# Projections of a dilated-attention step with written orders of loads, VectorE, ScalarE and TensorE

## The chip, the cores and the metric

The kernel runs on one core of a Trainium2 chip. The metric is the device time of one execution in microseconds, lower is better.

## The reference

One inference step of a decoder trunk of two layers over 512 prompt rows and 64 sample rows (8 sequences of 8 positions). The stage that matters here is the start of the first layer:

```python
h = rmsnorm(x, p['norm_mix'][i])
qkv = (h @ w_qkv).reshape(B, T, 3, N_DIL, N_HEAD_SLOTS, HEAD_DIM)   # 1024 -> 3 x 3 x 512
q = rope(rmsnorm(qkv[:, :, 0], q_gain), pos)
k = rope(rmsnorm(qkv[:, :, 1], k_gain), pos)
v = qkv[:, :, 2]
```

There are three head groups with window and dilation (128, 1), (512, 4) and (2048, 16). The sample rows also score against cached keys of each group (`cache_kv_w128`, `cache_kv_w512`, `cache_kv_w2048`). Attention, an output projection, a feed-forward block, a state-space layer and a second feed-forward block follow; they are not edited.

## The kernel before

All products are made in a split form: a weight tile `raw` is turned into a high part `whi` (a copy on ScalarE, L100) and a low part `wlo` (a subtraction on VectorE, L101), and three products on TensorE (high by high, low by high, high by low) add up to nearly full precision.

`qkv_phase` makes nine chunks of 512 columns: q2, k2, v2, q1, k1, q0, k0, v0, v1 (the digit is the group). A chunk is made by `qkv_chunk` in four steps (`kk`), each with a quarter of the depth: one weight load of 512 KB, one split, and 28 products of 512 columns into five accumulator banks (four of prompt rows, one of sample rows). The steps are numbered 0 to 35 by `turn[0]`. Behind each of the five groups of products of a step is a slot, `slot()`, where work that was put off with `later(n, fn)` is issued, n slots after it was asked for.

After a q or k chunk, the banks are evicted and scaled by ScalarE (L573; the sample rows by `sample_rows`, L377 and L378), squares (L577) and sums (L578) give the roots (L119 and `newton`, L110 to L114), and `finish(t)` rotates one of five row tiles on VectorE (L589, L591, L592). `turned(t)` then transposes it on TensorE (L604) and copies it out (L610). The rotations are spread over the next chunk's steps by `LATE` and `LAST`.

Beside this, cached keys are scored for the sample rows. Group 2 works by VectorE: for each of 32 pairs (sequence, part), `products` loads a key tile and a broadcast query tile from the scratch `qscr` and multiplies and reduces them (L409, L410); after four parts `Close2.turn` transposes the result into the score bank `Sd` (L427, L430) and VectorE adds the mask (L432). Groups 1 and 0 work by TensorE: `Score.turn` transposes one key unit (L516), ScalarE copies it (`ks`, L518), and `Score.dots` multiplies (L527, L532) into `Sd`, followed by VectorE's mask step (L534). `Sd` has one buffer, the transposes' bank `pt` two, the key copies `ks` two, and the cached tiles `kc` six.

The order on each engine comes from a planner that orders instructions by its own estimates of their times, except where `keep_in_program_order` ties an instruction to the one tied before it on the same engine. In the kernel before, the products and transposes on TensorE are tied from step 20 on (`PINNED`), and nothing else in this stage is. `PLAN` says behind which step the cached pairs and scores are asked for: in `step()`, at the end of a step, the tiles are loaded and their work is issued at once.

## Time and profile before

| | us |
|---|---|
| median of 3 runs | 1535.78 (1533.81 to 1536.32) |
| profiled execution, its own time | 1540.19 |
| span of the profiled execution | 1538.4 |
| first product of the second chunk | 40.48 |
| last product of the stage starts | 332.7 |

In the rows that follow, a timeline row has the start, the duration, the engine, the line of the code, the operation, what it writes and reads, and in brackets the engine's idle time before it with what ended it. A row of stretches has the stretch, its length, then for TensorE, its weight loads, VectorE, ScalarE and GpSimd the busy time and the number of instructions, the granted TensorE clock, the busy share of the DMA engines and GB/s; where it was asked for one line of the code, it has that line's engines alone. A row of groups has busy time and mean duration in ns, then idle time before, and a row of waits has who waited for whom, the total, the number and the longest. A row of DMA issues has the count, the size and the median time to landing.

### The profile page before, as it was taken

How to read it: one execution, taken by the hardware profiler on the slowest of the kernel's cores; microseconds unless marked ns; L12 is line 12 of the kernel's file. 1: busy time of each engine (PE TensorE's matmuls, PEld its weight loads, DVE VectorE, ACT ScalarE, POOL GpSimd, SP SyncE). 2: the span in 40 equal slices, each digit the busy share in tenths (PEclk: the TensorE clock that was granted, in tenths of full speed). 3: DMA queues.
4: the chain of work that ended last, by engine and by line, in shares of the span. 5: the costliest groups of instructions: out<-in, count | busy, mean ns of one | idle time of the engine just before them, and what ended most of it. 6: DMA issues, size and time to landing. Idle time of an engine off the chain costs nothing. (4 is left out here: it accounts for less than half of the span.)

```text
span 1538.4 us, 29552 instructions
## 1 busy us (share of the span) xinstructions
PE 1485.8 (97%) x12406; PEld 1391.0 (90%) x12406; DVE 902.7 (59%) x1507; ACT 521.2 (34%) x790; POOL 321.3 (21%) x368
## 2 busy tenths in 40 slices
PE   9999897898999999999999999999999999999998
PEld 7778675666799999999999999999999999999998
DVE  5899776444556954488789567853543333333342
ACT  4533444445544221222222353532332212221222
POOL 2012231220012107554344330030110001000100
PEclk9999999899999999999999999999999999999999
DMA  7599466788965655778766947965556555442222
GB/s 258 189 347 324 124 223 208 221 293 299 313 185 192 219 198 192 246 262 285 246 226 212 328 138 220 292 198 172 192 191 217 191 190 190 148 147 83 83 68 77
DMA packets 190493, 322.63 MB, mean 210 GB/s; under 512 B 39480, under 2 KB 137016, under 8 KB 188824
## 3 DMA queue, kind: packets, MB, share of 16 engines
q1 hardware_dynamic: 182888, 303.76, 58.9%
q10 hardware_dynamic: 4992, 10.04, 1.9%
q0 software_dynamic: 2480, 6.95, 1.2%
q8 instruction: 97, 1.59, 0.4%
q14 instruction: 36, 0.29, 0.1%
HBM read 289.22 MB, written 118.78 MB: 265 GB/s over the span
## 5 line engine op out<-in xcount | busy, mean ns | idle before, releaser
L101 DVE TENSOR_TENSOR wlo<-raw,whi 128x1024 fp32r<-128x1024 f32 x200 | 247.7, 1238 | 251.7 <-ACT whi L100 248.2
L100 ACT ACTIVATE whi<-raw 128x1024 fp32r<-128x1024 f32 x200 | 208.1, 1042 | 526.3 <-PE acc L107 407.6
L107 PE MATMUL acc<-xgl,whi 128*128 128x288 f32 x1760 | 379.0, 296 | 1.0 <-DVE xgl L172 1.0
L107 PE MATMUL acc<-xgh,wlo 128*128 128x288 f32 x1760 | 377.3, 295 | 0.0
L107 PE MATMUL acc<-xgh,whi 128*128 128x288 f32 x1760 | 377.1, 296 | 0.1
L107 PEld LDWEIGHTS acc<-xgl,whi 128*128 128x128 f32 x1760 | 282.6, 188 | 2.5 <-DVE xgl L172 1.3
L107 PEld LDWEIGHTS acc<-xgh,wlo 128*128 128x128 f32 x1760 | 282.9, 188 | 0.8 <-DVE wlo L101 0.4
L107 PEld LDWEIGHTS acc<-xgh,whi 128*128 128x128 f32 x1760 | 281.5, 188 | 0.7 <-DVE gt L906 0.3
L908 POOL TENSOR_TENSOR gt<-gt,rstd 128x576 f32<-128x576 f32 x44 | 77.2, 1756 | 430.4 <-ACT gt L907 430.3
L107 PE MATMUL acc<-hh,whi 128*128 128x288 f32 x704 | 151.3, 296 | 0.0
L107 PE MATMUL acc<-hh,wlo 128*128 128x288 f32 x704 | 151.1, 295 | 0.0
L107 PE MATMUL acc<-hl,whi 128*128 128x288 f32 x704 | 150.9, 295 | 0.0
L338 PE MATMUL acc<-wlo,xh 128*128 128x512 f32 x288 | 114.5, 399 | 2.8 <-DVE wlo L101 2.8
L338 PE MATMUL acc<-whi,xh 128*128 128x512 f32 x288 | 113.4, 415 | 1.3 <-ACT xh L277 1.1
L107 PEld LDWEIGHTS acc<-hh,wlo 128*128 128x128 f32 x704 | 113.0, 188 | 0.2 <-issue 0.2
L107 PEld LDWEIGHTS acc<-hl,whi 128*128 128x128 f32 x704 | 112.9, 188 | 0.2 <-issue 0.2
L107 PEld LDWEIGHTS acc<-hh,whi 128*128 128x128 f32 x704 | 113.0, 188 | 0.0
L338 PE MATMUL acc<-whi,xl 128*128 128x512 f32 x288 | 112.6, 398 | 0.0
L192 POOL TENSOR_TENSOR ssum<-ssum,sq 128x576 f32<-128x576 f32 x21 | 35.8, 1703 | 235.9 <-ACT sq L191 235.9
L338 PEld LDWEIGHTS acc<-wlo,xh 128*128 128x128 f32 x288 | 55.6, 193 | 14.5 <-DVE wlo L101 4.3
L338 PEld LDWEIGHTS acc<-whi,xh 128*128 128x128 f32 x288 | 55.2, 193 | 12.9 <-ACT xh L277 1.7
L409 DVE TENSOR_TENSOR kc<-kc 128x1024 f32<-128x1024 f32 x32 | 39.0, 1219 | 45.9 <-DMA kc<-qscr 45.9
(361 smaller groups left out, 1951.5 us busy)
## 6 DMA issues: line engine op xcount, KB each, us to landing
o_kv_s<-cache_kv_w SPq DMA_DIRECT2D x64, 1020.0 KB, 7.3
kc<-cache_kv_w SPq DMA_DIRECT2D x96, 512.0 KB, 5.8
raw<-ffn_w_gate SPq DMA_DIRECT2D x44, 512.0 KB, 4.1
raw<-ffn_w_up SPq DMA_DIRECT2D x44, 512.0 KB, 3.8
raw<-ffn_w_down SPq DMA_DIRECT2D x40, 512.0 KB, 3.5
raw<-w_qkv SPq DMA_DIRECT2D x36, 512.0 KB, 5.5
kc<-qscr SPq DMA_DIRECT2D x32, 512.0 KB, 6.1
o_kv_s<-cache_kv_w SPq DMA_DIRECT2D x16, 1008.0 KB, 6.1
```

The costliest lines, as they stand in the source:

```text
L100: s.activation(hi, raw, AF.Copy)
L101: mark[0] = v.tensor_tensor(lo, raw, hi.bitcast(F32), OP.subtract)
L107: te.matmul(ps[:, c, :HN], w, x[:, c * HN:(c + 1) * HN], start=first and i == 0, stop=last and i == 2)
L192: g.tensor_tensor(self.ss, self.ss, sq, OP.add)
L338: ins = nc.tensor.matmul(*a, **kw)
L409: eng.tensor_tensor(kc, kc, qb, OP.mult)
L908: g.tensor_tensor(t, t, nin.r, OP.mult)
```

## The change

The order on SyncE's loads, VectorE, ScalarE and TensorE in this stage is written out. `v` and `s` are wrapped in `Kept`, so that each of their instructions is tied in program order; TensorE is tied from the second chunk on; the loads of weights and cached tiles are tied too. What a step issues ahead of its products stands in a new function `begin()`:

1. the weight load of two steps ahead, the cached pairs of the next step, the key tiles of this step's scores (and in step 34 the next stage's values and masks);
2. the split of the next step's weights;
3. the work listed for the step: in the first step after a q or k chunk the roots and the first rotated tile, then the other rotations;
4. the products of the pairs whose tiles were asked for a step ago.

`Score` objects are made at the end of the step, from tiles that are already asked for. The squares and sums move from the eviction of a chunk to step 3 of this list. The table `PLAN` becomes `PAIRS` and `SCORES`, with some pairs at other steps (none in steps 8, 16, 17 and 20, two in 12 to 15 and 32 to 34). `turned(t)` comes 9 - t // 2 slots after the start of the step of its rotation, `Close2.turn` 10 slots after the start of its step. The store to `qscr` goes from SyncE's queue to GpSimd's.

```diff
-LATE, LAST = (2, 1, 1, 1), (2, 2, 1, 0)
-PLAN = {5: (2,), 6: (2,), ... 12: (2, 2), 13: (2,), 14: (2, 2), ... 20: (2,), 21: (1, 2), ... 32: (0, 0, 2, 2), 33: (0, 2), 34: (0, 0, 2)}
+CHUNKS = ((0, 2), (1, 2), (2, 2), (0, 1), (1, 1), (0, 0), (1, 0), (2, 0), (2, 1))
+LATE, LAST = (1, 2, 1, 1), (2, 2, 1, 0)
+PAIRS = {6: 1, 7: 1, 9: 1, 10: 1, 11: 1, 12: 2, 13: 2, 14: 2, 15: 2, 18: 1, 19: 1, 21: 1, ... 31: 1,
+         32: 2, 33: 2, 34: 2}
+SCORES = {21: (1,), ... 28: (1,), 29: (0,), 30: (0,), 31: (0,), 32: (0, 0), 33: (0,), 34: (0, 0)}
...
+    kept = tc.keep_in_program_order
+    v, s = Kept(tc, v), Kept(tc, s)
...
+    def begin():
+        j = turn[0]
+        if 4 <= j + 2 < 36:
...
+            kept(nc.sync.dma_start(raw, dram(A["w_qkv"], ...)))
+            raws.append(raw)
+        due = [ready.pop(0) for _ in range(PAIRS.get(j, 0))]
+        for _ in range(PAIRS.get(j + 1, 0)):
+            b, part = fill[2].pop(0)
+            kc = cache_tile(nc, A, kst, "kc", 2, b, 2 * part, 2, 0, kept)
+            qb = kst.tile([128, 2, 512], F32, name="kc")
+            kept(nc.sync.dma_start(qb, dram(qscr, ...)))
+            ready.append((b, part, kc, qb))
+        for gi in SCORES.get(j, ()):
+            b, n = fill[gi].pop(0), UNITS[gi]
+            cached.append((gi, b, [cache_tile(nc, A, kst, "kc", gi, b, c0, min(2, n - c0), 0, kept) for c0 in range(0, n, 2)]))
+        if j in notes:
+            notes[j]()
+        if j < 4:
+            split(j)
+        if j >= 3:
+            split(j + 1)
+        for fn in works.pop(j, ()):
+            fn()
+        for b, part, kc, qb in due:
...
+            v.tensor_tensor(kc, kc, qb, OP.mult)
+            v.tensor_reduce(...)
+            if part == 3:
+                later(10, Close2(nc, L, v, dk, psd, "Sd", prods.pop(b), b).turn)
+        return splits.pop(0)
...
+        def roots():
+            sh = wk.tile([128, 5, 8], F32, name="sh")
+            v.memset(sh[64:128, 4], 1.0)
+            for t in range(5):
+                pp = 128 if t < 4 else 64
+                sq = wk.tile([128, 8, 64], F32, name="t1")
+                s.activation(sq[:pp].rearrange("p h d -> p (h d)"), at[t][:pp], AF.Square)
+                v.tensor_reduce(sh[:pp, t], sq[:pp], AX.X, OP.add)
+            rsqrt(rq, sh, 1.0 / HD)
...
-            if turn[0] < PINNED:
-                turned(t, a, pp)
-            else:
-                later(4, lambda: turned(t, a, pp))
+            if (gi, part, t) == (2, 0, 4):
+                g.dma_start(qscr, a[:64])
+            later(9 - t // 2, lambda: turned(t, a, pp))
...
+        order = [4, 0, 1, 2, 3]
+        works[turn[0]] = [roots]
+        for i, n in enumerate(LATE if turn[0] < 28 else LAST):
+            works.setdefault(turn[0] + i, []).extend((lambda t=order.pop(0): finish(t)) for _ in range(n))
...
+    def values():
+        nc.sync.dma_start(vt0, L["vtscr"].rearrange("t p c -> p t c"))
+        nc.sync.dma_start(mp, A["c_mp"])
+
+    notes[34] = values
```

## The prediction

> **What bounds the kernel now.** I read the page's head first, then the stretches of the stage that the diff touches, then TensorE's waits inside that stage, and the timeline where a wait ended.

> ```profile
> span 1538.4 us, 29552 instructions
> PE 1485.8 (97%) x12406; PEld 1391.0 (90%) x12406; DVE 902.7 (59%) x1507; ACT 521.2 (34%) x790; POOL 321.3 (21%) x368
> 40.48:332.90 292.42, 230.44 (x896) 167.45 (x896) 0.96 0.71 239
> 97.86:127.42 29.56, 28.75 (x147) 22.69 (x146) 28.62 (x36) 10.58 (x16) 11.72 (x15) 1.00 1.03 378
> 154.28:198.98 44.70, 39.28 (x233) 30.51 (x232) 33.73 (x50) 22.33 (x37) 11.42 (x24) 0.92 0.42 125
> 242.74:293.55 50.81, 41.40 (x328) 32.02 (x327) 34.68 (x51) 19.14 (x30) 12.29 (x27) 0.90 0.64 204
> ```

> TensorE is the bound (97% of the span), so the change is worth what it takes from TensorE's lost time. All of it lies between 40.48 us, when the second chunk's products start, and 332.9 us, just behind the start of the last product of the stage: the third row counts 896 projection products there, 32 steps of 28. The first chunk keeps its order. Behind 332.9 us nothing is edited, and that part shifts as a block.

> How long would 292.4 us be without a wait? Rows of the timeline give the pieces.

> ```profile
> 170.16 0.39 PE L338 MATMUL acc<-wlo,xh 128*128 128x512 f32 x1
> 173.83 0.39 PE L338 MATMUL acc<-whi,xl 128*128 128x512 f32 x1
> 243.98 0.40 PE L338 MATMUL acc<-whi,xl 128*128 128x512 f32 x1
> 244.21 0.60 PE L516 MATMUL pt<-ident,kc 128*128 128x128 f32 x4
> 244.88 0.40 PE L338 MATMUL acc<-wlo,xh 128*128 128x512 f32 x1
> 220.87 1.06 ACT L100 ACTIVATE whi<-raw 128x1024 fp32r<-128x1024 f32 x1
> 231.09 1.06 ACT L100 ACTIVATE whi<-raw 128x1024 fp32r<-128x1024 f32 x1
> ```

> Between the first two rows lie 16 products: 3.67 / 16 = 0.229 us each, so a bare step is 28 x 0.229 = 6.4 us. Four transposes put between products cost 244.88 - 243.98 - 2 x 0.229 = 0.44. A step with one group-1 score and one rotated tile takes 231.09 - 220.87 = 10.2, so such a score costs 10.2 - 6.4 - 0.44 = 3.4. A group-0 score has one unit instead of four, about 1.0; closing a product tile about 0.5 (estimates from the former). The clean stage: 32 x 6.4 + 30 rotated tiles x 0.44 + 8 x 3.4 + 8 x 1.0 + 8 x 0.5 = 257 us. So some **35 us** are lost now, and that is the most that any order can win (1501 us). Where they go:

> ```profile
> PE Sd L427 <- DVE mx L534: 9.6, 2, 8.4
> PE acc L338 <- DVE a L378: 5.3, 1, 5.3
> PE pt L604 <- DVE a L592: 5.1, 4, 2.6
> DVE kc L409 <- DMA kc<-qscr: 45.9, 18, 7.1
> 86.15 0.49 PE L338 MATMUL acc<-wlo,xh 128*128 128x512 f32 x1 [1.61 <-DVE wlo L101]
> 87.19 0.39 PE L338 MATMUL acc<-whi,xl 128*128 128x512 f32 x1
> 87.41 0.39 PE L338 MATMUL acc<-wlo,xh 128*128 128x512 f32 x1
> 176.03 0.43 PE L604 MATMUL pt<-ident,a 64*128 64x64 f32 x4 [1.82 <-DVE a L592]
> 178.98 0.63 PE L338 MATMUL acc<-whi,xh 128*128 128x512 f32 x1
> 179.41 0.63 PE L338 MATMUL acc<-wlo,xh 128*128 128x512 f32 x1
> 305.34 0.76 PE L338 MATMUL acc<-whi,xsp 128*128 128x512 f32 x1 [5.29 <-DVE a L378]
> 309.75 0.53 PE L338 MATMUL acc<-whi,xh 128*128 128x512 f32 x1
> ```

> VectorE stands 45.9 us at cached products whose operands have not landed, and what TensorE needs (a mask step, a sample row, a rotated tile) is queued behind. Idle time has a second price: after 1.82 us idle the products come every 0.43 us instead of 0.23, and after 5.29 us they stay so until 309.75, 4.4 us in which about 2.0 are lost. After 1.61 us idle they come every 0.22.

> **The change, part by part.**

> *Loads a step earlier, splits first.* The products' two tiles are asked for one step (over 6.4 us) ahead, and VectorE reaches products last in its step. That takes the 45.9 us wait nearly away, and with it the 9.6 and 5.3 above. Work on each engine stays the same, operation by operation; so does the DMA traffic. A step's split waits only for the products two steps back, so it is ready unless VectorE lags a step: I cost it at nothing. VectorE needs per chunk 5 rotations, 4 splits, the roots and 2 to 4 products, some 28 to 32 us, against 27 to 40 of TensorE; if a chunk runs over, the next split is late by the excess. The query store moves from SyncE's queue to GpSimd's, once, ahead of the first products; nothing on TensorE waits for it. The next stage's values and masks are now asked for in step 34, behind its key tiles:

> ```profile
> mp<-c_mp SPq DMA_DIRECT2D x1, 512.0 KB, 7.8
> ```

> Even asked for 6 us into that step, the masks land by 14; the stage ends 16 after the step's start (two steps of 7.5 to 8). Nothing, while that cover holds; up to 3 us if the tiles ahead are late.

> *ScalarE's order is now written.* Here I see the largest cost. Durations:

> ```profile
> L101 DVE TENSOR_TENSOR wlo<-raw,whi 128x1024 fp32r<-128x1024 f32 x32 | 38.9, 1214 | 15.0 <-ACT whi L100 14.9
> L589 DVE TENSOR_TENSOR u<-a,C 128x1024 f32<-128x1024 f32 (+1 forms) x30 | 36.2, 1206 | 0.2
> L592 DVE TENSOR_TENSOR a<-a,rq 128x512 f32<-128x512 f32 (+1 forms) x30 | 19.6, 682 | 0.1
> L578 DVE TENSOR_REDUCE sh<-t 128x8 f32<-128x512 f32 (+1 forms) x30 | 19.8, 676 | 5.4 <-ACT t L577 5.1
> L518 ACT ACTIVATE ks<-pt 128x512 f32<-128x512 f32 x40 | 23.8, 598 | 48.7 <-PE pt L516 48.7
> L573 ACT ACTIVATE a<-acc,rr 128x512 f32<-128x512 f32 x23 | 15.6, 688 | 6.3 <-PE acc L338 5.7
> L119 ACT ACTIVATE sq<-sh,eps 128x40 f32<-128x40 f32 x6 | 1.9, 323 | 7.5 <-DVE sh L578 7.5
> 58.19 1.88 DVE L592 TENSOR_TENSOR a<-a,rq 64x512 f32<-64x512 f32 x3
> 36.77 0.19 DVE L110 RECIPROCAL rr<-sq 128x5 f32<-128x5 f32 x1
> 37.60 0.17 DVE L114 TENSOR_TENSOR rr<-rr,sq 128x5 f32<-128x5 f32 x1
> 245.82 0.69 ACT L377 ACTIVATE t<-acc,rr 64x512 f32<-64x512 f32 x1 [2.96 <-DVE sh L578]
> 246.53 1.08 ACT L518 ACTIVATE ks<-pt 128x512 f32<-128x512 f32 x2
> 247.18 0.81 PE L527 MATMUL Sd<-ks,Qz 128*32 128x128 f32 x12 [0.98 <-ACT ks L518]
> ```

> At the start of a chunk that follows q or k, begin() writes on ScalarE: the next split's high half, five squares, the square root; only then come the copies that the slots of that step ask for. The squares share two buffers with VectorE's sums, so the third waits for a sum, and the root waits for all five. In steps 24 and 28 the first of these copies is the fourth key unit of a score, and the dot products in slot 2 need it. Count from the last product of the chunk. The key turn of the last slot is copied by 0.44 + 0.60 = 1.1; four evictions (0.69 each) follow, the first done at 1.8, so TensorE, free at 0.4 and in need of bank 0, idles 1.4. The evictions end at 3.9, the sample half (0.69) at 4.6, the high half (1.06) at 5.6, VectorE's low half (1.21) at 6.8, five sums of 0.68 at 10.2, the root at 10.5, the key copy at 11.1. TensorE has by then run 12 products and a turn (1.8 + 2.7 + 0.44 = 5.0): idle 6.1. With 2.0 of slow products behind it a place costs 1.4 + 6.1 + 2.0 = 9.5, less some 0.5 because successive operations overlap by about 0.08 (three of 0.682 take 1.88): **9.0, twice: 18**. The last three rows above show the same queue at work in the kernel before: the sample half waits 2.96 us for a sum, the key copies come behind it, and TensorE idles 0.98 (the lower end; the upper is 9.5 with a lag of VectorE on top). I take the count, since now three operations more stand ahead of the copy.

> [...]

> *Rotations behind the roots.* In each of steps 4, 8, 16 and 20 the same chain ends, without a key turn ahead of it, about 1.5 us sooner: roots' sums at 7.6, square root, reciprocal and four short steps (37.77 - 36.77 = 1.0) by 9.0, and the first rotated tile (1.21 + 2 x 0.68) at 11.5. Its turn is fixed at the second slot of the next step, where TensorE arrives at 6.4 + 0.44 + 12 x 0.229 = 9.6. Idle 1.9 at four places: 7.6. Three of the four are long enough for the slow products that the row at 176.03 shows (seven or so at 0.43 for 0.23, 1.5 each): 4.5. **12** together. Ends: 0 where VectorE runs a little faster than the means, 20 where it lags 2 us more.

> *One score bank.* Closing a score and opening the next share one bank; VectorE's mask step is now queued behind the whole step's work, products included. In six steps (22, 25, 26, 29, 33, 35) the next dot products wait for it, 0.7 to 1.5 us each: **5** (ends 0 and 15, by the 9.6 that this same wait costs now).

> *Six buffers for loads.* Where two product pairs a step meet two group-0 scores (step 32), a score's tile is asked for only when a pair has been used, some 6 us into the step, and lands 6.5 us later:

> ```profile
> kc<-cache_kv_w SPq DMA_DIRECT2D x9, 256.0 KB, 6.5
> ```

> Its turn comes at 7.4 + 2.7 = 10.1: 2.2 idle and 1.5 slow, **4** (ends 0 and 8).

> Sum of the losses: 18 + 12 + 5 + 4 = 39, and 1 at the second chunk's first bank, 40 against 35 now. With the values in the middle of the small terms I take **+6 us**. The profiled execution took 1540.19 us, 1.8 more than its span and 4.4 above the median of the three times, 1535.78; it would take 1546, and the median 1535.78 + 6 = **1542 us**.

> [...]

> **The rivals.**
> - *No change, 1536 (1533 to 1539).* The second-slot stalls come out at 1.6 us or less; the row at 86.15 shows no slow products after 1.61. Then 6 us of slow products fall off. Its point is between 1.61 and 1.82.
> - *Faster, 1522.* The key copies in steps 24 and 28 do not stand behind the roots, so that the 18 us are not paid: 1542 - 18 = 1524, and 1522 with the bank's idle half gone. It decides at about 6 us per place (half of a 12 us gain); for it speaks that only 0.98 us were paid at this queue before, against it that the squares then ran while banks were still closing.
> - *All waits gone, 1505.* Four fifths of the 35 us are won. Against it stand four separate places above.
> - *Transfers, 1552.* Steps 12 to 15 now use two pairs a step, 2 x 1 MB and 0.5 MB of weights in 6.4 us, 400 GB/s, where the row at 97.86 shows a share of 1.03 at 378. If pairs land late by 4 us a chunk, VectorE starts the next roots so much later, twice with slow products: +10.

> **How the numbers follow.** Forecast (+3 to +12) 0.40, transfers 0.12, no change 0.16, faster 0.24, all gone 0.08. What a measurement here can tell from no change is about 0.2%, 3 us. Slower 0.52, same 0.16, faster 0.32. The range of 8 in 10 leaves the outer parts: 1518 to 1554. The likeliest case alone spans 1539 to 1548.

> **What would show it.** The stage between the second chunk's first product and the last would be 298 us for 292. TensorE's waits: score dots on the key copy, two of about 6 us; the rotated tile's turn on VectorE's last rotation step, four of about 2; VectorE on the query tiles' DMA under 10 us for 45.9. I am wrong if the two long waits on the key copy are missing (then 1522), or if VectorE still waits for query tiles tens of us (then 1552).

## The result and the profile after

The changed kernel takes 1555.54 us (median of 4 runs, 1553.50 to 1558.15) against 1536.05 us before in the same comparison: ratio 1.0126, 95% interval 1.0103 to 1.0150. It is slower by 19.5 us. The forecast was 1542 and its range ended at 1554: the direction holds, the size does not.

Its profiled execution took 1555.32 us. The head of its page:

```profile
span 1553.5 us, 29525 instructions
PE 1487.2 (96%) x12406; PEld 1392.7 (90%) x12406; DVE 912.5 (59%) x1507; ACT 520.4 (33%) x790; POOL 322.1 (21%) x369
```

Every engine is busy for what it was before, within 10 us; as many matmuls run. The difference is idle time and clock. The stage, from the second chunk's first product to the last, with TensorE's busy time, its weight loads, the granted clock, DMA share and GB/s (products alone, L337 in this kernel for L338):

```profile
39.98:346.20 306.22, 234.78 (x896) 170.03 (x896) 0.94 0.66 231
```

306.2 us for 292.4, at a mean clock of 0.94 for 0.96; 298 was forecast. TensorE's waits from 30 to 370 us (total, times, longest). L678 is every tied instruction of VectorE and ScalarE, L553 the score dots, L542 the turn of a cached key, L620 the turn of a rotated tile:

```profile
PE Sd L553 <- ACT ks L678: 10.7, 2, 5.4
PE Sd L553 <- DVE mx L678: 8.2, 7, 2.0
PE pt L620 <- DVE a L678: 5.7, 3, 2.0
PE pt L542 <- DMA kc<-cache_kv_w: 4.9, 2, 3.6
PE pt L620 <- issue: 3.2, 1, 3.2
PE acc L337 <- ACT a L678: 2.6, 2, 1.3
```

These six rows are the four losses of the forecast: the key copies (first and last row, 13.3 us at steps 24 and 28), the score bank (8.2), the first rotated tile (5.7 + 3.2 = 8.9, in steps 5, 9, 17 and 21; for the 3.2 the profile names no releaser, but that rotation ends on VectorE at 52.47 us and its turn begins at 52.57), the last cached keys (4.9). And the wait that the change was to take away is gone; VectorE on its query tiles, 45.9 us before:

```profile
DVE kc L678 <- DMA kc<-qscr: 2.4, 4, 1.2
```

ScalarE's timeline at step 24 shows the queue in front of a key copy (start, duration, form, count, idle before it):

```profile
202.13 2.42 ACT L678 ACTIVATE a<-acc,rr 128x512 f32<-128x512 f32 x4
204.56 0.69 ACT L678 ACTIVATE t<-acc,rr 64x512 f32<-64x512 f32 x1
205.15 1.05 ACT L678 ACTIVATE whi<-raw 128x1024 fp32r<-128x1024 f32 x1
206.10 1.14 ACT L678 ACTIVATE t<-a 128x512 f32<-128x512 f32 x2
208.31 1.22 ACT L678 ACTIVATE t<-a 128x512 f32<-128x512 f32 x2 [1.07 <-DVE sh L678]
209.70 0.63 ACT L678 ACTIVATE t<-a 64x512 f32<-64x512 f32 x1 [0.16 <-DVE sh L678]
211.07 0.33 ACT L678 ACTIVATE sq<-sh,eps 128x40 f32<-128x40 f32 x1 [0.74 <-DVE sh L678]
211.42 0.60 ACT L678 ACTIVATE ks<-pt 128x512 f32<-128x512 f32 x1
```

Its other end, on TensorE:

```profile
212.07 0.66 PE L553 MATMUL Sd<-ks,Qz 128*32 128x128 f32 x8 [5.36 <-ACT ks L678]
```

Four evictions, the sample half, a split, five squares paced by VectorE's sums, the root, and only then the copy: it ends 9.9 us behind the first eviction's start; the prediction's list gave 10.0 from there. The order of this queue was read rightly.

### The profile page after: what moved, and what is told of

The parts are those of the page before. It is cut to its first block, busy times and chain, and to the rows that moved or that the text cites. A ratio compares the mean times of both kernels' runs of the same rounds, so it can differ in the third digit from the quotient of the medians.

```text
span 1553.5 us, 29525 instructions
## 1 busy us (share of the span) xinstructions
PE 1487.2 (96%) x12406; PEld 1392.7 (90%) x12406; DVE 912.5 (59%) x1507; ACT 520.4 (33%) x790; POOL 322.1 (21%) x369
## 3 DMA queue, kind: packets, MB, share of 16 engines
q8 instruction: 97, 1.59, 0.4%
## 5 line engine op out<-in xcount | busy, mean ns | idle before, releaser
L101 DVE TENSOR_TENSOR wlo<-raw,whi 128x1024 fp32r<-128x1024 f32 (+1 forms) x168 | 207.6, 1236 | 240.7 <-ACT whi L100 237.4
L100 ACT ACTIVATE whi<-raw 128x1024 fp32r<-128x1024 f32 (+1 forms) x168 | 174.6, 1039 | 457.9 <-PE acc L107 397.0
L337 PE MATMUL acc<-whi,xh 128*128 128x512 f32 x288 | 121.8, 425 | 4.9 <-ACT a L678 2.6
L337 PE MATMUL acc<-wlo,xh 128*128 128x512 f32 x288 | 116.2, 405 | 0.0
L337 PE MATMUL acc<-whi,xl 128*128 128x512 f32 x288 | 115.5, 407 | 0.0
L192 POOL TENSOR_TENSOR ssum<-ssum,sq 128x576 f32<-128x576 f32 x21 | 36.2, 1725 | 233.5 <-ACT sq L191 233.5
L337 PEld LDWEIGHTS acc<-whi,xh 128*128 128x128 f32 x288 | 56.5, 196 | 17.0 <-ACT a L678 3.7
L337 PEld LDWEIGHTS acc<-whi,xl 128*128 128x128 f32 x288 | 56.5, 196 | 12.7
L337 PEld LDWEIGHTS acc<-wlo,xh 128*128 128x128 f32 x288 | 56.7, 197 | 10.1
## 6 DMA issues: line engine op xcount, KB each, us to landing
kc<-cache_kv_w SPq DMA_DIRECT2D x96, 512.0 KB, 6.2
raw<-ffn_w_gate SPq DMA_DIRECT2D x44, 512.0 KB, 3.8
raw<-ffn_w_up SPq DMA_DIRECT2D x44, 512.0 KB, 3.7
raw<-ffn_w_down SPq DMA_DIRECT2D x40, 512.0 KB, 3.4
raw<-w_qkv SPq DMA_DIRECT2D x36, 512.0 KB, 6.2
kc<-qscr SPq DMA_DIRECT2D x32, 512.0 KB, 6.2
```

Of the source, the lines that this page charges most:

```text
L100: s.activation(hi, raw, AF.Copy)
L101: mark[0] = v.tensor_tensor(lo, raw, hi.bitcast(F32), OP.subtract)
L192: g.tensor_tensor(self.ss, self.ss, sq, OP.add)
L337: ins = nc.tensor.matmul(*a, **kw)
```

## The experiments

All are edits of the changed kernel; gains are differences of medians to its 1555.54 us, ratios are to the kernel before, with 95% intervals. The kernel before, run beside each group, had medians of 1536.05 to 1538.02 us, so a gain is known to some 2 us. Line numbers shift with an edit.

### One wait at a time

**e1, keys first.** In steps 24 and 28 roots, rotations and products are written behind the second slot, and so behind the key copy and the mask step that stand there.

```diff
+        if j in (24, 28):
+            off[0] = 2          # later turns keep their slot
+            later(2, rest)      # rest: works of the step, then products
+        else:
+            rest()
```

> In steps 24 and 28 the roots, the rotations and the products are written behind the second slot of the step instead of ahead of its products, so that on ScalarE the fourth key copy and on VectorE the score's mask step come before them; all else is the changed kernel. Queue theory (TensorE loses time because what it needs stands behind the roots in a queue): the two waits of 5.4 us on the key copy and most of the 3.5 us of slow products behind each go, 12 to 16 us in all: 1540 to 1544 us. Rival (VectorE's total work binds the stage, a wait removed turns up at the next place): less than 5 us, 1551 or more, with a longer wait at the rotated tiles of the same chunk.

**e2, turn late.** The first rotated tile is turned four slots later.

```diff
-            later(9 - t // 2, lambda: turned(t, a, pp))
+            later(11 if t == 4 else 9 - t // 2, lambda: turned(t, a, pp))
```

> The first rotated tile's turn on TensorE comes 11 slots after its step's start instead of 7; nothing else moves. Queue theory: the waits of 3.2, 2.0, 1.7 and 2.0 us in steps 5, 9, 17 and 21 go, and with three of them the slow products behind them (13 us at half clock, 6 us lost): 13 to 15 us, 1541 to 1543 us. Rival (VectorE binds): the next step's split is late by the same time instead, under 4 us, 1552 or more.

**e3, ScalarE free.** `v, s = Kept(tc, v), Kept(tc, s)` becomes `v = Kept(tc, v)`.

> ScalarE's instructions of the stage are not tied; loads, VectorE and TensorE stay tied. Queue theory: the planner may put the fourth key copy ahead of the roots, the evictions ahead of the last key copy: the 5.4 and 1.3 us waits in steps 24 and 28 go, 12 to 18 us: 1538 to 1544 us. Rival (the order of VectorE and TensorE alone makes the loss): no change beyond 3 us.

**e5, two halves of a bank.** The score bank is allocated as 2 x 136 columns, and a score takes the halves in turn.

> The one bank of the scores becomes two halves of a bank, used in turn; nothing else moves. Theory (each wait is the front of the same queue: VectorE is behind its written order at the heads of the chunks of steps 24 and 28, so a wait taken away shows up at the next place): the waits of the score dots on the mask step (8.2 us over seven places) go, but most of the time comes back at the key copies and the first rotated tiles; 3 to 6 us gained, about 1551. Rival (the waits add up, each worth its idle time and the half clock behind it): 8.2 us of idle and about 4 of half clock go, 1543 to 1545.

Measured: e1 1551.40 us, ratio 1.0094 (1.0058 to 1.0131), 4.1 gained; e2 1548.72, 1.0077 (1.0053 to 1.0101), 6.8 gained; e3 1551.21, 1.0096 (1.0059 to 1.0134), 4.3 gained; e5 1550.04, 1.0093 (1.0074 to 1.0112), 5.5 gained. The intervals of e1, e3 and e5 overlap that of the changed kernel (1.0103 to 1.0150), so these three gains are not clear of noise one by one. In e1, e2 and e3 the wait aimed at is all but gone, and another has grown. TensorE's wait for the mask step (L566 is e1's line of the dots, L691 its tied instructions) in e1:

```profile
PE Sd L566 <- DVE mx L691: 11.9, 6, 5.2
```

The same in e2, with the wait for a split that is new there:

```profile
PE Sd L553 <- DVE mx L678: 10.1, 7, 4.0
PE acc L337 <- DVE wlo L678: 3.3, 4, 2.1
```

And in e3:

```profile
PE Sd L553 <- DVE mx L678: 13.3, 6, 6.9
```

8.2 us became 11.9, 10.1 and 13.3. In e1 the longest, 3.1 and 5.2 us, lie in steps 25 and 29, one step behind the edited ones. The forecast's rival that taking the key copies from behind the roots alone returns 18 us falls: the dots meet the next late thing, VectorE's mask step of the score before. Of the 12 to 18 us that the first theory expected of e1, e2 and e3, a quarter to a half came back. The halves of e5 did not part the bank: e8 below shows dots that still start, at 274.55 us, behind the mask step of the score before, at 274.11, so what an independent second bank would bring is left open; its 5.5 us are what the theory expected, but its rows do not explain them: the mask steps are 6.1 us for 8.2, and the changed kernel's own second execution (e17 below) has 5.9; the key copies are 10.7 as before.

### Loads asked in their own step

**e4.** The pair tiles are asked for in the step that uses them; products still stand last.

```diff
-        for _ in range(PAIRS.get(j + 1, 0)):
+        for _ in range(PAIRS.get(j, 0)):
...
+        due = [ready.pop(0) for _ in range(PAIRS.get(j, 0))]    # behind the loads
```

> The cached pairs' tiles are asked for in the step that uses them, not a step ahead; all else is the changed kernel. Theory (the early loads are what takes VectorE's wait on query tiles from 45.9 to 2.4 us): some 6 us from issue to landing against 1 to 9 us of splits and rotations ahead of the products, so 2 to 5 us of wait at most of the 26 steps with pairs, 60 us in all on VectorE, of which TensorE feels a third: 1570 to 1580 us. Rival (the loads were hidden anyway): within 4 us of 1555.

Measured: 1555.96, ratio 1.0138 (1.0085 to 1.0191): no change, so the theory's 1570 to 1580 was wrong. The prediction gave the loads and the place of the products as one cause. VectorE's wait on query tiles is 12.8 us here, with one of 7.6; in e12 below, where the loads stay early and the products come forward, it is 44.6. So the place does most of it. On TensorE one wait of 7.6 us in step 33 (the close of a pair tile on the mask step) takes the place of the 4.9 us for key tiles:

```profile
DVE kc L678 <- DMA kc<-qscr: 12.8, 7, 7.6
PE Sd L407 <- DVE mx L678: 7.6, 1, 7.6
```

### Two and three at once

**e6** is e1 and e2, **e7** is e1 and e5, **e8** all three.

> Both of the earlier edits at once: in steps 24 and 28 the roots, rotations and products are written behind the score dots, and the first rotated tile is turned four slots later. Apart they gave 4.1 and 6.8 us. Theory (one queue): the sum of the two or a little less, 9 to 12 us, 1544 to 1547, with the waits of the dots on the score bank now the largest group, above 12 us. Rival (together they free the whole wait that each had hidden for the other): both predicted terms return, 18 + 12 us, 1526.

> The roots, rotations and products of steps 24 and 28 behind the score dots, and two halves of a bank for the scores. Theory (behind the key copies the score bank was the next thing late: taken alone each returns little, together they return the sum of both idle times with their half clock): stage 15 to 18 us shorter than the changed kernel's, about 1539, more than the two single gains together (4.1 and what the two halves alone give). Rival (what is late is VectorE's block of roots and rotations itself, 13 us at a chunk's head against a step of 10 us, so the next split or the turn waits instead): no more than the single gains together, 1547 to 1549.

> All three: dots ahead of the roots in steps 24 and 28, the first rotated tile turned four slots later, two halves of a bank for the scores. Theory (the three predicted terms, 18 + 12 + 5, are the whole loss apart from the loads): the stage ends 25 to 30 us earlier than in the changed kernel, 1526 to 1530, faster than the kernel before. Rival (VectorE's in-order work at the chunks' heads is the bound, whichever wait shows it): 1540 or more, not faster than before.

Measured: e6 1547.91, ratio 1.0067 (1.0041 to 1.0092); e7 1549.06, 1.0074 (1.0051 to 1.0097); e8 1544.52, 1.0045 (1.0018 to 1.0073). e6 gained 7.6 us, less than either theory or rival of it, e7 6.5, at the edge of its rival, and e8 11.0, as its rival had it. TensorE's wait for the mask step is its largest row in all three, 14.7, 11.9 and 15.2 us. VectorE's timeline of e8 in step 29 shows why:

```profile
268.52 0.69 DVE L700 TENSOR_TENSOR a<-a,rq 128x512 f32<-128x512 f32 x1
269.13 1.22 DVE L700 TENSOR_TENSOR u<-a,C 128x1024 f32<-128x1024 f32 x1
270.38 0.69 DVE L700 TENSOR_TENSOR a<-u 128x512 f32<-128x512 f32 x1
271.11 0.69 DVE L700 TENSOR_TENSOR a<-a,rq 128x512 f32<-128x512 f32 x1
271.72 1.22 DVE L700 TENSOR_TENSOR kc<-kc 128x1024 f32<-128x1024 f32 x1
272.97 1.22 DVE L700 TENSOR_REDUCE P<-kc 128x16 f32<-128x1024 f32 x1
274.11 0.29 DVE L700 CUSTOM_DVE_ANT_0 Sall<-Sd,md 128x136 f32<-128x136 f32 x1
```

TensorE at the same place: the dots that the mask step reads, and the next ones:

```profile
263.49 0.22 PE L580 MATMUL Sd<-kT,Qz 128*32 128x8 f32 x8
274.55 1.08 PE L575 MATMUL Sd<-ks,Qz 128*32 128x128 f32 x16 [5.62 <-DVE mx L700]
```

The score is complete at 263.7. Its mask step takes 0.29 us, but is issued at 274.11, behind a split (at 265.41), two rotations and a pair's products, all written ahead of it, and the next score waits 5.62 us. Untying or moving the key copies cannot help that; the mask step itself has to be written earlier.

### The mask step ahead of the block

**e9.** In steps 21 to 30 roots, rotations and products are written behind the third slot, one behind the score's mask step, and the close of a pair tile comes 8 slots after the start of its step instead of 10.

```diff
+        if j in range(21, 31):
+            off[0] = 3
+            later(3, rest)
...
-                later(10, Close2(...).turn)
+                later((8 if j >= 21 else 10) - o, Close2(...).turn)
```

> In steps 21 to 30 everything of a step that is not a split or a score (roots, rotations, products) is written behind the score's mask step on VectorE and behind its key copies on ScalarE; the pair's closing turn is put two slots earlier. Theory (the dots wait because the mask step stands at the end of VectorE's written order, behind a block of up to 13 us): the waits of the dots on the mask step in steps 24, 25, 28, 29 (above 5 us in the earlier runs) and on the key copies go together; about 9 us, 1546 or a little less. Rival (the block is simply too long for its steps: the next split then waits for VectorE): 1551 or more, with waits of the projection on wlo above 5 us.

**e10** is e9 with the first rotated tile turned three slots later.

> The same, and the first rotated tile turned three slots later. Theory: 15 to 17 us less than the changed kernel, 1538 to 1541, with no wait over 3 us left in steps 4 to 30 but the 1.3 us at the head of a chunk on its first bank. Rival (VectorE's block is the bound): 1544 or more, as with the three edits together before.

**e11** is e10 with bank t - 1 evicted behind the slot of bank t in a chunk's last step, and score tiles asked for ahead of pair tiles.

```diff
+            if out is not None and kk == 3 and t:
+                out(t - 1, ps)      # ScalarE evicts and scales bank t - 1
```

> The same, and: the four evictions of a query or key chunk written among its last products, as each bank closes, and score tiles asked ahead of pair tiles. Theory: the 1.3 us at the chunk's head go, as does part of the 5 us for the last cached keys; 20 us less than the changed kernel, 1526 to 1535, no slower than the kernel before. Rival: 1540 or more; then what is left is not in these waits, and the stage's products themselves or what follows the stage carry it.

**e15** is e11 with rotations one, one, two, one over a chunk's steps and the close of step 21 at its old slot.

> All places as before, the close of the fourth pair tile at its old slot, and rotations one, one, two, one over the four steps in place of one, two, one, one. Theory (what is left is VectorE's block behind the roots in the second step of a chunk): the wait of a turn in steps 11 and 17 and the one of 2.3 us in step 22 go, 3 to 6 us less than all places alone: 1522 to 1525. Rival: the fourth and fifth rotated tiles now wait instead, 1528 or more.

**e12.** VectorE is not tied (`s = Kept(tc, s)` alone).

> VectorE is not tied to the written order any more, ScalarE, SyncE and TensorE are. Theory (the written order of VectorE is what makes the waits on the mask step and on the rotated tiles, 8.2 + 8.9 us of idle): those two groups shrink below 6 us together; 8 to 12 us less, 1544 to 1547. Rival (it is ScalarE's order, or TensorE's own): the same as the changed kernel within 4 us.

Measured: e9 1541.72, ratio 1.0029 (1.0008 to 1.0050), 13.8 gained; e10 1532.01, 0.9961 (0.9948 to 0.9974), 23.5 gained; e11 1528.06, **0.9928 (0.9904 to 0.9952)**, 27.5 gained; e15 1527.71, 0.9942 (0.9923 to 0.9962). e9 and e10 gained more than expected, e11 what was expected. So e10, e11 and e15 beat both kernels, e11 by some 10 us against the kernel before; e15 brought nothing on top: the close put back to its old slot has its mask step behind two rotations and a pair's products again (0.29 us at 183.15), and a score waits 5.1 us for it, so what its other rotations are worth alone is not shown. In e9's profiled execution, the slowest of ten, no wait for a mask step is among the first rows; half of the key copies' wait is left (L566 dots, L633 turn of a rotated tile):

```profile
PE pt L633 <- DVE a L691: 6.9, 3, 2.9
PE pt L555 <- DMA kc<-cache_kv_w: 5.8, 2, 3.5
PE Sd L566 <- ACT ks L691: 5.3, 4, 2.5
```

e1 moved the block past the mask step in two steps and gained 4, and the wait came up one step behind; e9 moved it in ten steps and gained 14. Where e1 had rotations and products of step 25 ahead of the mask step and TensorE waited 3.1 us, e9 has it straight behind the split, and TensorE does not wait:

```profile
224.24 0.29 DVE L691 CUSTOM_DVE_ANT_0 Sall<-Sd,md 128x136 f32<-128x136 f32 x1
```

The key copies and the close of a pair tile move with it in e9, so the 14 us are not the mask step's alone. In e11 the stage, with waits of 4.9 us (key copies) and 3.3 us (one mask step) as its longest rows:

```profile
39.90:322.70 282.80, 231.77 (x898) 167.17 (x896) 0.96 0.72 248
```

e12 went the other way: 1588.88, ratio 1.033 (1.030 to 1.036), 33 us slower than the changed kernel. Its longest waits, of TensorE and then of VectorE (L609 is the last step of a rotation, L515 the product):

```profile
PE pt L620 <- DVE a L609: 35.6, 3, 15.7
```

```profile
DVE kc L515 <- DMA kc<-qscr: 44.6, 20, 6.8
```

Left to the planner, products come ahead of roots and rotations again and VectorE stands 44.6 us at their tiles, as it did before; but TensorE's turns are now tied to a slot and wait up to 15.7 us for it. The expectation of a gain was wrong: with TensorE's slots as they are, VectorE's written order as a whole is worth more than the planner's.

### The terms of the sum

**e13.** Squares, sums and two of three operations of each rotation are left out.

> Leaves out the squares and sums of the roots and the first two of the three operations of every rotation, so VectorE and ScalarE have 14 us less per query or key chunk; TensorE runs every product, turn and dot as before. It measures the first term, the clean stage, on its own. Theory (the clean stage was right at 257 us, the losses were too small): the stage, 306.2 us in the changed kernel, falls to 258 to 268, the loads for the last cached keys being all that is left of the waits. Rival (the clean stage was put too short, and the miss of the sum lies there): 275 or more though no wait of rotations, mask steps or key copies is left.

**e14.** Transposes that nobody reads are put ahead of the waiting dots.

```diff
+            if us == (2, 3) and turn[0] in (24, 28):
+                z = ptp.tile([128, 4, 128], F32, name="pt")
+                for i in range(10):     # 40 transposes into z
...
```

> Forty transposes into a spare bank of the turns are put ahead of the score dots that wait for a key copy in steps 24 and 28 (nobody reads them), so that TensorE works, at most 5 us, where it stood idle for 5.4. Theory (slow products are the price of idle time, 6.8 us at half clock behind each of the two waits): the two half-clock stretches go, 3.4 us each less something for the dots coming later; 4 to 7 us less, 1549 to 1551. The term in the sum was 2.0 at each place. Rival (the slow stretch comes from something else than idle time, or the added work delays the dots as much as it saves): the same as the changed kernel within 2 us, or slower.

The stage of e13:

```profile
40.18:314.90 274.72, 226.10 (x896) 163.94 (x896) 0.99 0.75 258
```

Its largest waits:

```profile
PE pt L542 <- DMA kc<-cache_kv_w: 5.2, 2, 4.0
PE Sd L553 <- ACT ks L670: 3.7, 2, 1.8
PE acc L337 <- ACT a L670: 2.6, 2, 1.3
...
PE Sd L553 <- DVE mx L670: 2.1, 4, 0.5
```

It took 1522.36 us in one execution. The stage, 274.7, is at the rival's figure, but its condition, no waits left, is not met. Of the last row one wait of 0.5 lies behind the last product; the others make 5.2 + 3.7 + 2.6 + 1.6 = 13.1 us idle, and two half-clock stretches of 3.4 us in the stage cost 1.6 each (worked out below): 274.7 - 16.3 = 258.4. The clean stage was put at 257. That term holds.

e14: 1555.57, ratio 1.0130 (1.0102 to 1.0157): no change, though the two waits are 1.0 us for 5.4 (L558 the dots, L555 the added transposes):

```profile
207.77 4.53 PE L555 MATMUL pt<-ident,kc 128*128 128x128 f32 x40
213.66 0.43 PE L558 MATMUL Sd<-ks,Qz 128*32 128x128 f32 x8 [1.00 <-ACT ks L683]
```

Where the changed kernel's products ran at a clock of 0.50 until 215.8, these ran at 1.00, so the idle time, 5.36 us there, is what halved it (the first half of the theory). But the stage ended only 1 us earlier: at step 28 the next wait for a mask step is 2.94 us where it was 1.42, and the first turn of step 17, which no edit touched, waited 3.5 for 1.7. So taking these slow products away did not shorten the kernel. In the changed kernel they measure 3.3 us (below) where the sum had 4.0, and the miss does not lie there.

### The base

> The kernel before, unchanged, once more, for a second profiled execution: the one that the prediction counted from (1540.2 us) lay 4.1 us above the median of all its runs (1536 to 1538). Theory (the 4 us were chance in the stage of the projections, whose cached products wait for transfers): this execution takes about 1536 and its stage 287 to 290 us for 292.4, the part behind it the same within 1 us. Rival (they lie behind the stage): the stage 291 to 294 again, the rest of the span shorter or longer.

> The changed kernel, unchanged, once more. Theory (its order is written, so its stage hardly varies): stage 306 us within 2, time 1553 to 1558. Rival (the first turns and mask steps vary as much as the sums they are made of): 3 us or more away from 306.

> The kernel before a third time: as for the second, stage 287 to 290 us where the time is near 1536; the three executions together show how far the stage alone carries its spread.

The kernel before took 1536.79 and 1535.98 us, the changed one 1552.87. Stage of the kernel before, second execution, then third, then of the changed kernel's second:

```profile
40.41:330.40 289.99, 229.95 (x896) 166.88 (x896) 0.96 0.71 241
```

```profile
40.01:329.10 289.09, 229.18 (x896) 166.44 (x894) 0.96 0.71 241
```

```profile
39.99:349.00 309.01, 237.31 (x896) 172.36 (x896) 0.93 0.67 230
```

290.0 and 289.1 where the prediction counted from 292.4: most of the 4 us by which that execution lay above the median were in the stage. The changed kernel's stage varied as well, 306.2 and 309.0, against the expectation of 2 us. Two of its rows in the second execution:

```profile
PE pt L620 <- DVE a L678: 6.3, 3, 2.4
PE Sd L553 <- DVE mx L678: 5.9, 8, 1.8
```

The second row is 2.3 us shorter than in the first execution, with no edit. The others are 10.7 and 2.6 (key copies), 3.2 (first turn) and 5.5 (key tiles).

## Why the prediction was wrong, point by point

| | predicted | first execution | second execution |
|---|---|---|---|
| clean stage | 257 | 258.7 (306.2 - 47.5) | 258.6 (309.0 - 50.4) |
| key copies behind the roots | 18 | 13.3 idle + 3.3 slow = 16.6 | 13.3 + 4.7 = 18.0 |
| first rotated tile's turn | 12 | 8.9 + 6.1 = 15.0 | 9.5 + 9.0 = 18.5 |
| one score bank | 5 | 8.2 + 1.6 = 9.8 | 5.9 + 0 = 5.9 |
| loads of the last cached keys | 4 | 4.9 + 1.6 = 6.5 | 5.5 + 3.0 = 8.5 |
| bank of the second chunk | 1 | 0 | 0 |
| losses | 40 | 48 | 51 |

Both executions are of the changed kernel. The idle times are the rows of the waits above; one of 0.5 us for the score bank lies behind the stage's last product, so 47.5 and 50.4 count in the stage. "Slow" is TensorE's work inside the half-clock stretches that follow these waits, times 0.47, since a product takes 0.43 us for 0.23. The first execution has seven (52.0 to 58.8, 86.1 to 89.5, 144.1 to 147.5, 209.0 to 215.8, 232.9 to 236.3, 263.6 to 270.4, 321.6 to 325.0 us), the second eight (51.5 to 58.3, 85.6 to 89.1, 143.7 to 150.5, 177.8 to 181.2, 211.9 to 218.8, 266.6 to 273.4, 321.2 to 324.6, 334.8 to 338.2 us).

- *The mechanism* was right: the 45.9 us at query tiles go, and the written order gives back more than that won. All four places were where the prediction put them, the two waits on the key copy to 0.7 us, and the clean stage holds to 2 us.
- *The steps that failed* are terms of the sum of losses, 48 and 51 us for 40. The first rotated tile's turn was put at 12 and measures 15.0 and 18.5; its first wait is 3.2 us instead of 1.9, with 6.8 us of half clock behind it. The loads of the last cached keys were put at 4 and measure 6.5 and 8.5. "One score bank" was put at 5, all of it idle, and measures 9.8 in the first execution and 5.9 in the second, so on that term the two differ as much as the forecast misses. All idle time was put at some 30 us (14, 7.6, 5, 2.2 and 1) and is 35.3 and 34.2; all slow products at 10 (4.0, 4.5 and 1.5) and are 12.6 and 16.7.
- *The mask step* was not overlooked, but its price depends on the other places. The prediction says that it is queued behind the whole step's work and puts 0.7 to 1.5 us on a place, where it had counted ScalarE's queue operation by operation. In the changed kernel as it stands that is not far off (0.5 to 2.0 us). It grows when the other places are repaired, to 11.9 us in e1, 14.7 in e6 and 15.2 in e8.
- *The base.* The difference was taken against a stage of 292.4 us and applied to the median; two further executions have 290.0 and 289.1. The means are 290.5 before and 307.6 for the changed kernel's two executions, 17.1 apart, of the 19.5 measured. So of the miss, 1.9 us are the base, and 9.6 that the changed kernel's stage is 307.6 for 298. The rest of the span carries no difference that these executions agree on (1246.0, 1245.0 and 1245.1 before; 1247.3 and 1242.1 after), so the last 2.4 are not assigned.
- *The sum as a method.* Terms that add up to the loss of one kernel do not say what removing each would bring: e1, e2 and e5 gained 4.1, 6.8 and 5.5 where the terms measure 16.6, 15.0 and 9.8. The rival "faster, 1522" took one term off the sum; e1 took it off in the kernel and got 4.1 us of the 18.
- *Rivals.* "Transfers, 1552" came nearest in time, for another reason: VectorE's wait for tiles was 2.4 us. "No change" falls with the four turns, none of them below 1.6 us, and with the half clock behind three of them (3.2, 2.0 and 1.7 us). In the rows of ScalarE at 202.13 to 211.42 the key copy comes where it is written, behind operations that waited 1.07, 0.16 and 0.74 us, and in e8 VectorE's mask step, 0.29 us long, starts at 274.11 behind all that is written ahead of it, its score complete at 263.7.

## What to carry to other kernels

When an order is written by hand, list for each short operation that another engine waits for (a mask step, a copy, an eviction) what stands ahead of it on its engine, and write it ahead of the long block; in e8 one operation of 0.29 us behind 10 us of work kept TensorE waiting for 5.6. A wait taken away returns its length only if the next thing in line is not late as well (e1 got 4.1 us back where the term measures 16.6): try the repairs together before one of them is called worthless. And take the base of a difference from several executions, since one stage of one execution was 2 to 3 us off its kind.

## What the runs showed of the hardware

```profile
85.28 0.46 PE L620 MATMUL pt<-ident,a 64*128 64x64 f32 x4 [1.97 <-DVE a L678]
190.09 0.64 PE L553 MATMUL Sd<-ks,Qz 128*32 128x128 f32 x16 [1.97 <-DVE mx L678]
```

The windows that hold them, each with the one behind it (the column before the last two is the granted clock):

```profile
82.70:86.10 3.40, 1.43 (x9) 0.90 (x8) 3.33 (x4) 0.51 (x2) 0.56 (x1) 1.00 0.00 0
86.10:89.50 3.40, 3.40 (x10) 2.62 (x9) 3.33 (x5) 0.06 (x1) 0.06 (x1) 0.50 0.14 39
188.50:191.90 3.40, 1.81 (x24) 1.51 (x25) 1.43 (x3) 0.48 (x1) 0.66 (x4) 1.00 0.92 308
191.90:195.30 3.40, 3.40 (x39) 2.66 (x38) 2.30 (x2) 1.67 (x3) 0.00 (x0) 1.00 0.97 340
```

The first lies inside one window, 1.43 us busy, and the next window runs at 0.50; the second crosses an edge, leaves 1.81 busy, and the next runs at 1.00. So 1.97 us idle of the 3.40 were enough here and 1.59 were not; between them it is not sharp (an idle 1.91 us within the window that ends at 174.87 was followed by full clock, 1.71 within the one that ends at 144.1 by half). The idle 1.91 us belong to a turn that stood idle 1.97 before 174.91, partly in the next window. In the second execution the same turn stood idle 1.97 before 176.82, all of it within the window that ends at 177.80, and half clock followed. So the prediction's point "between 1.61 and 1.82 us" was no property of the length alone: where the idle time falls on the grid decided with it.
